# Order of decoding, early rows and early expert blocks in a two-layer block kernel on one core

## The chip, the cores and the metric

The kernel runs on one core of a Trainium2 chip, as one launch. Its time is the device time in microseconds (us); before the change it is 2848.39 us, the median of three runs (2846.98 to 2852.76). The engines are called by their names in the profile: PE multiplies matrices, PEld loads its weights, DVE does elementwise work on vectors, ACT evaluates activations, POOL (GpSimd) issues indirect transfers, SP issues the other transfers. All five run their own instruction queues, each in a fixed order.

## The reference

Two transformer blocks over 512 tokens of width 1024, in float32. The part that matters is the end of the first block, a layer that picks experts by product keys:

```
ada = silu(c) @ w_ada + b_ada            # 6 x 1024: shift1 scale1 gate1 shift2 scale2 gate2
x   = x + gate1 * mix                    # mix: attention and convolution, then w_out
h2  = rms_norm(x) * (1 + scale2) + shift2
q   = h2 @ w_query                       # 8 heads, two halves of 128
s1, s2 = scores of both halves against 128 keys each; top 16 of each
cand = 16 x 16 sums; top 16 -> expert index idx = 128*e1 + e2, gates = softmax
a   = gelu(h2 . peer_u[idx])             # 16384 experts, 8*16 = 128 per token
out = sum_k gates * a * peer_v[idx]
x   = x + gate2 * out
```

The second block (a long convolution, neighbourhood attention, pooling, and 16 experts) follows and is not touched.

## The kernel before, in words

`ada` is kept as 48 columns of 128. The first 16 are made by PE at the start. The other 32 (groups 8 to 23 of two columns each) are made by DVE in `ada_late` (L209): a group is a load of 1 MB into one of two `wada` tiles, two products with the row of `c` summed along the line (L219), and an addition of the bias (L223). Groups 8 to 19 run behind the four convolution groups (L366). Groups 20 to 23, which are gate2 (columns 40 to 47), are read for the first time at the very end of the expert layer (L778); they run after the eighth output block of `w_out` (L387). An output block is 24 matmuls, a bias and gate on ACT (L380), an addition to X (L381), a square on ACT and a sum on POOL. After them comes the norm of X (`rms_t`, L122 and L127), the column `gs2` (L468, which reads columns 32 to 39) and `modulate` (L164), whose steps are L166 on DVE, L167 and L168 on ACT, L169 on DVE.

In `peer` (L400 on) the 512 tokens are four tiles of 128. Tiles 0, 1 and 2 (384 tokens, `TD`) are done densely: all 128 blocks of 128 experts are scored for them, and the scores are weighted with a matrix of gates that is mostly zero. Tile 3 is done by gathering: for each of its tokens the 128 chosen rows of `peer_u`, then of `peer_v`, come by indirect transfers, 256 in all, each of 128 rows of 4 KB (L651).

- A *u unit* scores one block: load (L434), split into two parts (ACT L437, DVE L438), 24 matmuls of 384 columns (`u_matmuls`), then a Gelu. Each of the two parts has two buffers, the load has four.
- `queries` (L495) makes scores and their top 16 per head. `decode(t)` (L515) turns them into indices and gates of tile t, mostly on DVE; it is a generator that yields ten times. For tile 3 it writes `gidx` (L582) and `ggate`, for the others the rows e1T, e2T and gT.
- `spread(t)` (L593) lays the gates of a dense tile out as a matrix in eight *blocks* of 16 tokens. A block is 16 comparisons on DVE (L600), two more (L604), two copies on ACT (L605), 32 matmuls of 128 columns on PE (L609), four copies back (L611) and two stores to `Gd` (L613). It is called here the spread stage: 24 blocks.
- `early_u` (L618) does u units ahead of the main loop, and stores their Gelu in `Ad`. The blocks for it are those e with e mod 16 in `AHEAD` (L30): 40 of 128. Ten go between the yields of `decode(0)`, one into the step behind each spread block, the remaining six behind the stage. In the same step two yields of `decode(t + 1)` are taken.
- The main loop runs over e = 0 to 127 with an order written out by hand: a *v unit* (18 matmuls of 512 columns, `v_matmuls`) for each e, a u unit for those not done ahead, and `pace`, which puts gather steps between them in proportion to the units done. A gather step is an indirect transfer on POOL and a sum on DVE (L658 for `peer_u`, L664 for `peer_v`). The rows have five buffers in the pool `rp`, which is opened behind the spread stage.

Outside the main loop a planner sets each engine's order: by its own model of time it gives an engine the first instruction in program order whose operands and buffers are ready. An engine then keeps that order whatever happens on the chip.

Of the kernel before, what the change touches and what calls it, by code (L numbers as in the profile page):

```python
# [9 lines left out]
F32 = mybir.dt.float32  # L10
# [4 lines left out]
AF = mybir.ActivationFunctionType  # L15
ALU = mybir.AluOpType
# [4 lines left out]
P = 128  # L21
D = 1024
# [3 lines left out]
NEG = -1e30  # L26
LOW = -3e38
NDT = 3
TD = NDT * P
AHEAD = (1, 4, 7, 10, 13)  # L30
MAGIC = 12582912.0
TWO_PI_HI = 6.28125
TWO_PI_LO = 2.0 * math.pi - 6.28125
# [2 lines left out]
def body(ctx, tc, I, O):  # L36
    nc = tc.nc
    mm = nc.tensor.matmul
    act = nc.scalar.activation
    vtt = nc.vector.tensor_tensor  # L40
    vts = nc.vector.tensor_scalar
    stt = nc.vector.scalar_tensor_tensor
# [33 lines left out]
    def cols_of(name):  # L76
        o, n = CO[name]
        return cols[:, o:o + n]
# [98 lines left out]
    with ExitStack() as fx:  # L177
# [31 lines left out]
        def ada_late(gs, ins):  # L209
            ws_ = []  # L210
            for g in gs:
                w = fp.tile([P, 2, D], F32, name="wada", tag="wada", bufs=2)
                nc.sync.dma_start(w, I["w_ada_l"][g - KD])
                ws_.append((g, w))
                if len(ws_) == 2 or g == gs[-1]:
                    with tc.issue_after(ins.ins):
                        for g_, w_ in ws_:
                            for j in range(2):
                                stt(w_[:, j], w_[:, j], 1.0, cb, op0=ALU.mult, op1=ALU.mult,  # L219
                                    accum_out=ada[:, 2 * g_ + j:2 * g_ + j + 1])  # L220
                    ws_ = []
            b0, b1 = 2 * gs[0], 2 * gs[-1] + 2
            vtt(ada[:, b0:b1], ada[:, b0:b1], cols_of("b_ada")[:, b0:b1], op=ALU.add)  # L223
# [8 lines left out]
        with ExitStack() as ex:  # L232
# [8 lines left out]
            homes = [(ep, "dw")] * 4 + [(pmk, "sq")] * 2 + [(fp, "k_sb"), (fp, "v_sb"), (pmk, "sx")]  # L241
# [22 lines left out]
            for k in range(KD):  # L264
                if k + 2 < KD:
                    ada_group(k + 2, aw[k + 2])
                if k + 4 < KD:
                    aw.append(ada_load(k + 4))
                stt(gs1[:, k:k + 1], ada[:, 2 * k + 1:2 * k + 2], 1.0, cols_of("norm1_g")[:, k:k + 1],
                    op0=ALU.add, op1=ALU.mult)  # L270
# [101 lines left out]
        for i in range(KD):  # L372
            ps = mmp()
            hi, lo = wo.get(i)
            n = 0
# [3 lines left out]
            t = fp.tile([P, T], F32, name="mt", tag="mt", bufs=2)  # L379
            act(t, ps, AF.Identity, bias=gb1[:, i:i + 1], scale=ada[:, 16 + i:17 + i])  # L380
            ins = vtt(X[:, i], X[:, i], t, op=ALU.add)  # L381
# [2 lines left out]
                nc.gpsimd.tensor_copy(sx, sq)  # L384
            elif i < KD - 1:
                ptt(sx, sx, sq, op=ALU.add)
        ada_late(range(20, 24), ins)  # L387

    upx = ExitStack()
    up = upx.enter_context(tc.tile_pool(name="up", bufs=2))  # L390
    with ExitStack() as px:
        peer(px, tc, I, locals())
# [9 lines left out]
def peer(px, tc, I, E):  # L402
    nc = tc.nc
    mm = nc.tensor.matmul
    act = nc.scalar.activation
    vtt = nc.vector.tensor_tensor
    vts = nc.vector.tensor_scalar
    stt = nc.vector.scalar_tensor_tensor
# [9 lines left out]
    htm = kp.tile([P, D], F32, name="htm", tag="htm")  # L418
    gidx = kp.tile([P, P], I32, name="gidx", tag="gidx")
    ggate = kp.tile([P, P], F32, name="ggate", tag="ggate")  # L420
    e1T = kp.tile([P, TD], F32, name="e1T", tag="e1T")
    e2T = kp.tile([P, TD], BF16, name="e2T", tag="e2T")
    gT = kp.tile([P, TD], F32, name="gT", tag="gT")
    gs2 = kp.tile([P, KD], F32, name="gs2", tag="gs2")
    NBK = TD // 16
    Gd = [drp.tile([P, NBK, 64, 16], F32, name=f"Gd{c}") for c in range(2)]
    up = E["up"]
    papp = px.enter_context(tc.tile_pool(name="papp", bufs=2, space=PSUM))
    EARLY = [e for e in range(P) if e % 16 in AHEAD]
    Ad = drp.tile([len(EARLY), P, TD], F32, name="Ad")  # L430

    def u_split(e, lo_engine):
        raw = up.tile([P, KD, P], F32, name="uraw", tag="uraw", bufs=4)
        nc.sync.dma_start(raw, I["peer_uT"][e])  # L434
        hi = up.tile([P, KD, P], F32R, name="uhi", tag="uhi")
        lo = up.tile([P, KD, P], F32R, name="ulo", tag="ulo")
        act(hi, raw, AF.Copy)  # L437
        lo_engine.tensor_tensor(lo, raw, hi.bitcast(F32), op=ALU.subtract)  # L438
        return hi, lo

    def u_matmuls(hi, lo):
        ps = papp.tile([P, TD], F32, name="aps", tag="aps")
        for k in range(KD):
            mm3(ps, hi[:, k], lo[:, k], hh[:, k, :TD], hl[:, k, :TD], k == 0, k == KD - 1)
        return ps

    with ExitStack() as qx:
        gp = qx.enter_context(tc.tile_pool(name="gp", bufs=2))
# [144 lines left out]
        def spread(t, step):  # L593
            for blk in range(8 * t, 8 * t + 8):
                st = gp.tile([P, P, 16], F32, name="st", tag="st")
                for hb in range(2):
                    c0 = 16 * blk + 8 * hb
                    of = gp.tile([P, 8, P], F32, name="of", tag="of")
                    for j in range(8):
                        vts(of[:, j], iop, e1T[:, c0 + j:c0 + j + 1], gT[:, c0 + j:c0 + j + 1],  # L600
                            op0=ALU.is_equal, op1=ALU.mult)
                    oq = gp.tile([P, 8, P], F32, name="oq", tag="oq")
                    ob2 = gp.tile([P, P, 8], BF16, name="ob2", tag="ob2")
                    vtt(ob2, iob, e2T[:, None, c0:c0 + 8].to_broadcast([P, P, 8]), op=ALU.is_equal)  # L604
                    act(oq.rearrange("p t e -> p e t"), ob2, AF.Copy)  # L605
                    for t4 in range(2):
                        ps = pp.tile([P, 4, P], F32, name="gps", tag="gps")
                        for j in range(4):
                            mm(ps[:, j], oq[:, 4 * t4 + j], of[:, 4 * t4 + j], start=True, stop=True)  # L609
                        o = 8 * hb + 4 * t4  # L610
                        act(st[:, :, o:o + 4], ps.rearrange("p t e -> p e t"), AF.Copy)  # L611
                for c in range(2):
                    nc.sync.dma_start(Gd[c][:, blk], st[:, 64 * c:64 * c + 64])  # L613
                step()
# [3 lines left out]
        def early_u(count):  # L618
            for n in itertools.islice(early, count):
                gl = up.tile([P, TD], F32, name="gle", tag="gle", bufs=2)  # L620
                act(gl, u_matmuls(*u_split(EARLY[n], nc.vector)), AF.Gelu)  # L621
                nc.sync.dma_start(Ad[n], gl)
# [2 lines left out]
            queries(h)  # L625
        for _ in decode(0):
            early_u(1)
        for t in range(NDT):
            dec = decode(t + 1)

            def step():
                early_u(1)
                for _ in itertools.islice(dec, 2):
                    pass

            spread(t, step)
            for _ in dec:
                pass

    early_u(len(EARLY))  # L640

# [1 line left out]
    rp = px.enter_context(tc.tile_pool(name="rp", bufs=1))  # L643
    outp = rp.tile([P, D], F32, name="gacc", tag="gacc")
    nc.vector.memset(outp, 0.0)
    ga = rp.tile([P, P], F32, name="ga", tag="ga")
    scr = rp.tile([P, D], F32, name="gscr", tag="gscr")

    def gather(src, j):
        row = rp.tile([P, D], F32, name="row", tag="row", bufs=5)  # L650
        nc.gpsimd.indirect_dma_start(out=row, out_offset=None, in_=I[src],  # L651
                                     in_offset=bass.IndirectOffsetOnAxis(ap=gidx[:, j:j + 1], axis=0))
        return row

    def gather_step(n):
        if n < P:
            row = gather("peer_u", n)
            stt(scr, row, 1.0, htm, op0=ALU.mult, op1=ALU.mult, accum_out=ga[:, n:n + 1])  # L658
        else:
            if n == P:  # L660
                act(ga, ga, AF.Gelu)
                vtt(ga, ga, ggate, op=ALU.mult)
            row = gather("peer_v", n - P)
            stt(outp, row, ga[:, n - P:n - P + 1], outp, op0=ALU.mult, op1=ALU.add)  # L664

    ppo = px.enter_context(tc.tile_pool(name="ppo", bufs=1, space=PSUM))
    acc = [[ppo.tile([P, T], F32, name=f"acc{t}{c}", tag=f"acc{t}{c}") for c in range(2)] for t in range(NDT)]
    GG = 8
# [33 lines left out]
    def v_matmuls(e, wh, wl, vh, vl):  # L702
        for t in range(NDT):
            for c in range(2):
                mm3(acc[t][c], wh[:, t * P:(t + 1) * P], wl[:, t * P:(t + 1) * P],
                    vh[:, c * T:(c + 1) * T], vl[:, c * T:(c + 1) * T], e == 0, e == P - 1)

    total = 2 * P - len(EARLY)
    done = [0, 0]

    def pace(units):
        done[0] += units
        while done[1] < 2 * P and done[1] * total < done[0] * 2 * P:
            gather_step(done[1])
            done[1] += 1

# [8 lines left out]
    def u_mm(e):  # L725
        if e < P and e not in EARLY:
            ups[e] = u_matmuls(*usp.pop(e))
            return True
        return False
# [34 lines left out]
    for c in range(2):  # L764
        for t in range(4):
            cs = slice(c * T, (c + 1) * T)
            if t < NDT:
                st = rp.tile([P, T], F32, name="ot", tag="row", bufs=5)
# [775 lines left out]
```

## Time and profile before

| | us |
|---|---|
| median of three runs | 2848.39 |
| profiled execution, its own time | 2849.08 |
| its span (first to last instruction) | 2847.3 |
| PE busy | 2582.1 (91%) |
| DVE busy | 1457.3 (51%) |
| ACT busy | 917.3 (32%) |
| POOL busy | 495.1 (17%) |

The span holds the first block's mixer up to about 272 us, the norm and the queries up to 402 us, decoding and the spread stage up to 663 us, a tail of u units to 703 us, the main loop to 1591 us, and the second block to the end. Busy time is the union of an engine's instructions. The granted clock is that of PE, 1.00 for 2.4 GHz and 0.50 for 1.2 GHz.

### The profile page before, as it was taken

How to read it: one execution, taken by the hardware profiler on the slowest of the kernel's cores; microseconds unless marked ns; L12 is line 12 of the kernel's file. 1: busy time of each engine (PE TensorE's matmuls, PEld its weight loads, DVE VectorE, ACT ScalarE, POOL GpSimd, SP SyncE). 2: the span in 40 equal slices, each digit the busy share in tenths (PEclk: the TensorE clock that was granted, in tenths of full speed). 3: DMA queues.
4: the chain of work that ended last, by engine and by line, in shares of the span. 5: the costliest groups of instructions: out<-in, count | busy, mean ns of one | idle time of the engine just before them, and what ended most of it. 6: DMA issues, size and time to landing. Idle time of an engine off the chain costs nothing. (4 is left out here: it accounts for less than half of the span.)

```text
span 2847.3 us, 32895 instructions
## 1 busy us (share of the span) xinstructions
PE 2582.1 (91%) x12609; PEld 1813.7 (64%) x12609; DVE 1457.3 (51%) x2907; ACT 917.3 (32%) x1368; POOL 495.1 (17%) x342
## 2 busy tenths in 40 slices
PE   7998999988999999999999899969878888788887
PEld 5666788988988898888888777633323223233332
DVE  4485899994777877878778865330101101011011
ACT  4363448984333333333333434220000000000001
POOL 0001000001444544445444213010000000000000
PEclk9998999999999999999999999989999999999999
DMA  6343324556898989889988422279999999999997
GB/s 249 120 155 126 104 97 180 203 199 231 291 319 314 319 311 325 314 312 313 330 301 316 158 96 80 111 301 429 427 428 427 427 428 427 428 428 428 427 428 303
DMA packets 195077, 826.41 MB, mean 290 GB/s; under 512 B 17159, under 2 KB 77447, under 8 KB 167144
## 3 DMA queue, kind: packets, MB, share of 16 engines
q1 hardware_dynamic: 154280, 680.67, 61.0%
q0 software_dynamic: 38016, 138.43, 13.7%
q10 hardware_dynamic: 2624, 5.22, 0.5%
q8 instruction: 99, 1.62, 0.2%
q14 instruction: 58, 0.48, 0.0%
HBM read 787.02 MB, written 37.22 MB: 289 GB/s over the span
## 5 line engine op out<-in xcount | busy, mean ns | idle before, releaser
L1353 DVE TENSOR_TENSOR sg<-sg,upp 128x512 f32<-128x512 f32 x32 | 22.0, 688 | 754.3 <-PE upp L1346 754.3
L85 PE MATMUL aps<-hh,uhi 128*128 128x384 f32 x1024 | 347.8, 340 | 8.9 <-ACT gle L621 8.9
L87 PE MATMUL aps<-hh,ulo 128*128 128x384 f32 x1024 | 345.7, 338 | 5.1 <-DVE ulo L438 5.1
L86 PE MATMUL aps<-hl,uhi 128*128 128x384 f32 x1024 | 345.6, 337 | 0.0
L1346 PE MATMUL upp<-wch,XB 128*64 128x512 f32 x1024 | 274.2, 625 | 50.9 <-DMA wch<-in_w_up 50.9
L651 POOL DMA_INDIRECT row<-in_peer_u,gidx x128 | 205.2, 1603 | 628.7 <-issue 386.2
L85 PE MATMUL acc<-vh,wh 128*128 128x512 f32 x768 | 299.8, 390 | 2.4 <-ACT wh L81 2.4
L87 PE MATMUL acc<-vh,wl 128*128 128x512 f32 x768 | 300.2, 391 | 0.0
L86 PE MATMUL acc<-vl,wh 128*128 128x512 f32 x768 | 299.6, 390 | 0.4 <-DVE vl L82 0.4
L1346 PE MATMUL gp<-wch,XB 128*64 128x512 f32 x1024 | 268.0, 608 | 34.2 <-DMA wch<-in_w_gate 34.1
L1372 PE MATMUL y<-wch,aT 128*64 128x512 f32 x1024 | 247.7, 598 | 11.9 <-ACT aT L1358 11.9
L651 POOL DMA_INDIRECT row<-in_peer_v,gidx x128 | 207.4, 1621 | 240.3 <-DVE gacc L664 209.4
L1346 PEld LDWEIGHTS upp<-wch,XB 128*64 128x64 f32 x1024 | 86.7, 143 | 211.2 <-issue 141.7
L1346 PEld LDWEIGHTS gp<-wch,XB 128*64 128x64 f32 x1024 | 84.1, 140 | 198.7 <-issue 145.2
L437 ACT ACTIVATE uhi<-uraw 128x1024 fp32r<-128x1024 f32 x128 | 135.7, 1060 | 211.2 <-DMA uraw<-in_peer_uT 160.8
L85 PEld LDWEIGHTS aps<-hh,uhi 128*128 128x128 f32 x1024 | 194.0, 189 | 13.9 <-ACT gle L621 10.5
L87 PEld LDWEIGHTS aps<-hh,ulo 128*128 128x128 f32 x1024 | 193.6, 189 | 6.1 <-DVE ulo L438 6.1
L86 PEld LDWEIGHTS aps<-hl,uhi 128*128 128x128 f32 x1024 | 194.1, 190 | 4.1
L438 DVE TENSOR_TENSOR ulo<-uraw,uhi 128x1024 fp32r<-128x1024 f32 x128 | 156.2, 1221 | 73.4 <-ACT uhi L437 72.8
L1372 PEld LDWEIGHTS y<-wch,aT 128*64 128x64 f32 x1024 | 85.5, 136 | 141.3 <-issue 123.0
L1352 ACT ACTIVATE sg<-gp 128x512 f32<-128x512 f32 x32 | 19.1, 597 | 482.5 <-PE gp L1346 482.5
L664 DVE SCALAR_TENSOR_TENSOR gacc<-row,ga,gacc 128x1024 f32<-128x1024 f32 x128 | 164.1, 1282 | 2.4
(405 smaller groups left out, 4277.9 us busy)
## 6 DMA issues: line engine op xcount, KB each, us to landing
wch<-in_w_gate SPq DMA_DIRECT2D x64, 2048.0 KB, 35.4
wch<-in_w_up SPq DMA_DIRECT2D x62, 2048.0 KB, 32.9
wch<-in_w_down SPq DMA_DIRECT2D x62, 2048.0 KB, 34.4
uraw<-in_peer_uT SPq DMA_DIRECT2D x128, 512.0 KB, 7.6
vraw<-in_peer_v SPq DMA_DIRECT2D x128, 512.0 KB, 6.9
Gd<-st SPq DMA_DIRECT2D x48, 512.0 KB, 3.6
gg<-Gd SPq DMA_DIRECT2D x16, 1536.0 KB, 17.4
wraw<-in_w_in SPq DMA_DIRECT2D x36, 512.0 KB, 3.2
```

The costliest lines, as they stand in the source:

```text
L85: mm(out, lh, rh, start=first, stop=False)
L86: mm(out, lh, rl, start=False, stop=False)
L87: mm(out, ll, rh, start=False, stop=last)
L437: act(hi, raw, AF.Copy)
L438: lo_engine.tensor_tensor(lo, raw, hi.bitcast(F32), op=ALU.subtract)
L651: nc.gpsimd.indirect_dma_start(out=row, out_offset=None, in_=I[src], in_offset=bass.IndirectOffsetOnAxis(ap=gidx[:, j:j + 1], axis=0))
L664: stt(outp, row, ga[:, n - P:n - P + 1], outp, op0=ALU.mult, op1=ALU.add)
L1346: mm(ps[64 * e:64 * e + 64], xT[:, k, 64 * e:64 * e + 64], gu[w][e][:, o:o + T], start=k == 0, stop=k == KD - 1)
L1352: act(sg, ps2[0], AF.Silu)
L1353: vtt(sg, sg, ps2[1], op=ALU.mult)
L1372: mm(y[c][64 * e:64 * e + 64], aT[:, fb, 64 * e:64 * e + 64], dn[e][:, o:o + T], start=fc == 0 and fb == 0, stop=fc == 3 and fb == 3)
```

## The change

Three things. The groups 20 to 23 of `ada` are put behind the output blocks 1 to 4, one each, in place of behind the last. The decoding order is 0, 1, 3, 2, and two yields of it are taken in every step until it ends; from then on each step also does four gather steps, up to 40, and what is left of the 40 is done behind the stage. These rows have two buffers of their own in a pool `gr` that is opened before the stage, and the product is written over the row. Each step does two u units; `AHEAD` holds the eight odd residues, so 64 of 128 blocks are scored ahead: ten beside `decode(0)`, 48 in the 24 steps, six behind. The main loop has 64 u units and 216 gather steps left, and `pace` counts accordingly.

```
+NGE = 40
-AHEAD = (1, 4, 7, 10, 13)
+AHEAD = (1, 3, 5, 7, 9, 11, 13, 15)
@@ output blocks
-        ada_late(range(20, 24), ins)
+            if 0 < i < 5:
+                ada_late([19 + i], ins)
@@ peer
+    gr = px.enter_context(tc.tile_pool(name="gr", bufs=1))
+    ga = gr.tile([P, P], F32, name="ga", tag="ga")
+    sums, homes = [], [(gr, 2)]
+    def gather(src, j):
+        pool, bufs = homes[-1]
+        row = pool.tile([P, D], F32, name="row", tag="row", bufs=bufs)
...
+    def gather_step(n):
+        if n < P:
+            row = gather("peer_u", n)
+            stt(row, row, 1.0, htm, op0=ALU.mult, op1=ALU.mult, accum_out=ga[:, n:n + 1])
...
+        def decodes():
+            for t in (1, 3, 2):
+                yield from decode(t)
+                ended.append(t)
+        dec = decodes()
+        early_rows = iter(range(NGE))
+        def step():
+            early_u(2)
+            for _ in itertools.islice(dec, 2):
+                pass
+            if 2 in ended:
+                for n in itertools.islice(early_rows, 4):
+                    gather_step(n)
         for t in range(NDT):
-            dec = decode(t + 1)
-            def step():
-                early_u(1)
-                for _ in itertools.islice(dec, 2):
-                    pass
+            while t and t not in ended:
+                next(dec, None)
             spread(t, step)
-            for _ in dec:
-                pass
+        for n in early_rows:
+            gather_step(n)
@@ in front of the main loop
+    sums.append(outp)
+    homes.append((rp, 5))
-    done = [0, 0]
+    done = [0, NGE]
-        while done[1] < 2 * P and done[1] * total < done[0] * 2 * P:
+        while done[1] < 2 * P and (done[1] - NGE) * total < done[0] * (2 * P - NGE):
```

## Rows read from the trace of the kernel before

**Rows 1.** Busy time by stage: start:end length, engines, granted clock, DMA share, GB/s

```profile
402.00:452.00 50.00, 41.69 (x225) 39.67 (x225) 48.66 (x229) 28.66 (x34) 0.00 (x0) 0.97 0.35 121
452.00:663.00 211.00, 191.60 (x1329) 183.63 (x1329) 193.54 (x656) 186.08 (x206) 0.00 (x0) 0.99 0.54 198
663.00:703.00 40.00, 33.73 (x184) 33.09 (x182) 10.47 (x10) 12.07 (x18) 4.97 (x5) 0.96 0.72 257
703.00:1591.00 888.00, 887.22 (x4389) 795.18 (x4390) 696.88 (x855) 327.11 (x432) 407.64 (x251) 1.00 0.89 310
```

**Rows 2.** Waits of PE, 452 to 663 us: total us, times, longest

```profile
PE gps L609 <- ACT oq L605: 10.2, 10, 1.5
PE gps L609 <- ACT st L611: 7.9, 9, 1.6
```

**Rows 3.** Waits of PE, 703 to 1591 us

```profile
PE acc L85 <- ACT wh L81: 2.4, 2, 1.9
```

**Rows 4.** Timeline of DVE, output blocks and norm: start, duration, idle before

```profile
249.29 1.23 DVE L82 TENSOR_TENSOR wlo<-wraw,whi 128x1024 fp32r<-128x1024 f32 x1 [3.71 <-ACT whi L81]
...
272.20 1.22 DVE L219 SCALAR_TENSOR_TENSOR wada<-wada,c 128x1024 f32<-128x1024 f32 x1
...
276.78 0.17 DVE L122 RECIPROCAL rt<-rt 128x4 f32<-128x4 f32 x1
...
279.12 1.28 DVE L166 TENSOR_TENSOR mt<-X,rps 128x512 f32<-128x512 f32 x2 [0.81 <-PE rps L127]
...
285.11 0.16 DVE L468 SCALAR_TENSOR_TENSOR gs<-ada,cols 128x8 f32<-128x8 f32 x1
```

**Rows 5.** Timeline of ACT, the same norm

```profile
274.88 0.26 ACT L121 ACTIVATE rt<-nps,eps_t 128x4 f32<-128x4 f32 x1 [1.87 <-PE nps L119]
285.31 1.52 ACT L167 ACTIVATE mt<-mt,ada,gs 128x512 f32<-128x512 f32 x2 [10.16 <-DVE gs L468]
```

**Rows 6.** Timeline of PE, first product of the queries

```profile
289.55 0.79 PE L85 MATMUL mmp<-hh,uhi 128*128 128x512 f32 x1 [10.46 <-ACT uhi L81]
```

**Rows 7.** Timeline of ACT, u units one behind the other

```profile
665.60 1.06 ACT L437 ACTIVATE uhi<-uraw 128x1024 fp32r<-128x1024 f32 x1 [3.24 <-PE aps L86]
666.57 0.47 ACT L621 ACTIVATE gle<-aps 128x384 f32<-128x384 f32 x1
669.76 1.06 ACT L437 ACTIVATE uhi<-uraw 128x1024 fp32r<-128x1024 f32 x1 [2.72 <-PE aps L86]
```

**Rows 8.** Groups of DVE, 452 to 663 us: busy us, mean ns, idle before

```profile
L600 DVE TENSOR_SCALAR of<-iop,e1T,gT 128x128 f32<-128x128 f32 x384 | 103.7, 341 | 9.2 <-PE gps L609 8.8
L604 DVE TENSOR_TENSOR ob<-iob,e2T 128x1024 bf16<-128x1024 bf16 x48 | 32.4, 685 | 2.8 <-ACT oq L605 2.8
L438 DVE TENSOR_TENSOR ulo<-uraw,uhi 128x1024 fp32r<-128x1024 f32 x24 | 29.2, 1218 | 1.9 <-ACT uhi L437 1.8
```

**Rows 9.** Timeline of DVE, places from decoding to the first gathered rows

```profile
450.88 1.21 DVE L566 TENSOR_TENSOR oh<-oh,wb__3955 128x2048 bf16<-128x2048 bf16 x1
...
642.91 0.22 DVE L582 CAST gidx<-ef 128x128 int32<-128x128 f32 x1
...
706.94 1.22 DVE L658 SCALAR_TENSOR_TENSOR gscr<-row,htm 128x1024 f32<-128x1024 f32 x1
...
708.20 1.23 DVE L658 SCALAR_TENSOR_TENSOR gscr<-row,htm 128x1024 f32<-128x1024 f32 x1
```

**Rows 10.** Timeline of POOL, a row issued before and in the main loop

```profile
669.18 1.11 POOL L651 DMA_INDIRECT row<-in_peer_u,gidx  x1 [366.40 <-issue]
...
708.44 1.80 POOL L651 DMA_INDIRECT row<-in_peer_u,gidx  x1 [33.07 <-DVE gscr L658]
```

**Rows 11.** Line 651, all 256 rows, issue to landing

```profile
DMA to landing us min/median/max: 4.9/8.0/10.3
```

**Rows 12.** Transfers issued 452 to 663 us: KB each, median us to landing

```profile
uraw<-in_peer_uT SPq DMA_DIRECT2D x24, 512.0 KB, 3.4
```

**Rows 13.** Transfers issued 1100 to 1200 us

```profile
uraw<-in_peer_uT SPq DMA_DIRECT2D x10, 512.0 KB, 8.4
```

More of the change, by code (lines that the diff above doesn't have):

```diff
@@ L445, in u_matmuls @@
         return ps
+    gr = px.enter_context(tc.tile_pool(name="gr", bufs=1))
[4 more added lines that the diff above has]
+        row = pool.tile([P, D], F32, name="row", tag="row", bufs=bufs)
+        nc.gpsimd.indirect_dma_start(out=row, out_offset=None, in_=I[src],
+                                     in_offset=bass.IndirectOffsetOnAxis(ap=gidx[:, j:j + 1], axis=0))
+        return row
+    def gather_step(n):
+        if n < P:
+            row = gather("peer_u", n)
+            stt(row, row, 1.0, htm, op0=ALU.mult, op1=ALU.mult, accum_out=ga[:, n:n + 1])
+        else:
+            if n == P:
+                act(ga, ga, AF.Gelu)
+                vtt(ga, ga, ggate, op=ALU.mult)
+            row = gather("peer_v", n - P)
+            stt(sums[0], row, ga[:, n - P:n - P + 1], sums[0], op0=ALU.mult, op1=ALU.add)
     with ExitStack() as qx:
@@ L627, in peer @@
             early_u(1)
-        for t in range(NDT):
-            dec = decode(t + 1)
-            def step():
-                early_u(1)
-                for _ in itertools.islice(dec, 2):
-                    pass
+        ended = []
+        def decodes():
[11 more added lines that the diff above has]
+                    gather_step(n)
+        for t in range(NDT):
+            while t and t not in ended:
+                next(dec, None)
             spread(t, step)
-            for _ in dec:
-                pass
+        for n in early_rows:
+            gather_step(n)
     early_u(len(EARLY))
@@ L645, in peer @@
     nc.vector.memset(outp, 0.0)
[L646 to L664, printed above, removed]
+    sums.append(outp)
+    homes.append((rp, 5))
     ppo = px.enter_context(tc.tile_pool(name="ppo", bufs=1, space=PSUM))
```

## Prediction, made before the change was run

> **What bounds the kernel now.** I read the busy time by stage first, since the change moves work from one stage to another. The reader is to see in it that the main loop has no room on PE (887.22 of 888 us busy) and the three stretches ahead of it have some: 8.3 us idle in 402 to 452, 19.4 in the spread stage, 6.3 in the tail, 34.0 together [rows 1]. In the spread stage DVE is busy 92% of the time and ACT 88%, so PE's room there is not free for the asking. Next come PE's own waits. In the stage they are for the two copies on ACT that stand before and behind the matmuls of the gates, not for the u units [rows 2]; in the main loop there are 2.4 us of them [rows 3]. Last I read the timelines around the norm, where the third part of the change acts: DVE's products for the last `ada` groups begin as soon as X is done, and everything behind them queues [rows 4]. The sums below go against the profiled execution's 2849.08 us, 0.7 above the median of the runs.
>
> **Part 1: the `ada` groups.** Eight products of about 1.15 us each stand on DVE between the last X and `gs2`. The sequence is: ACT has the square root at 274.88 + 0.26 = 275.14 [rows 5], but DVE takes the reciprocal only at 276.78, behind four products; the norm's row comes 2.34 us later, at 279.12; then four more products, so that `gs2` is there at 285.11 [rows 4]. ACT has waited 10.16 us for it [rows 5], and PE starts the queries at 289.55 [rows 6]. Without the products the reciprocal runs at 275.2, L166 at 277.5, its first half ends at 278.2, and L167 (half of 1.52, 0.76) and L168 (about 0.6) give PE its operand at 279.6: 9.9 us earlier. PE's wait in rows 6 ends on the split of the query weights. That load could not start before the last product either, if its buffers lie where `wada` was; with the products early it falls away too. I take -9.5. The ends are -11, should the two splits also leave ACT's way, and 0, should the loads hold something else up.
>
> The products now stand behind output blocks 1 to 4. A group costs DVE 2 x 1.15 + 0.2 = 2.5 us there, and DVE idles 3.71 us in such a block before the next weight split [rows 4], so they are hidden. Without that cover four blocks would be late by up to 2.5 us each, 10 in all, which is the 0 end. SP gets the four loads of `wada` between the loads of `w_out`; a group's buffer comes free two groups before, and a block lasts 5.6 us, so nothing behind them on SP should be late.
>
> **Part 2: 24 u units out of the main loop.** Two neighbouring units start 4.16 us apart when PE alone paces them [rows 7]. The loop, PE-bound, loses 24 x 4.16 = 99.8 us, and the spread stage gains the same 99.8 us of PE work. So the move itself is worth nothing; what counts is how much of the 34.0 us of idle PE is filled, and what new idle arises. The 24 stores and loads of `Ad` and the `uraw` loads go along with the units.
>
> The spread stage afterwards: PE 191.6 + 99.8 = 291 us. DVE 193.5 + 24 x 1.22 + 40 rows x 1.26 (706.94 to 708.20) [rows 9] = 273. ACT 186.1 + 24 x (1.06 + 0.47) = 223 [rows 7]. PE is now the longest by 18 us, where before the three were within 8 us. A second u unit in each step also gives PE something to run while it waits for ACT's copies. I take it that the idle falls from 19.4 to about 8, a gain of 11, with ends of 0 (same idle) and 28 (all of the stage's, and most of the other stretches'). The other stretches I leave as they are: beside `decode(0)` DVE is 97% busy, and the tail runs the same six units.
>
> The rest of the main loop: 310 GB/s x 888 us = 275 MB move there now. The change takes out 24 loads of 0.524 MB and 40 rows of the same size, and adds 24 reads of 0.197 MB: 246 MB in 788 us, 313 GB/s, as before. Without the 40 rows it would be 339. So I cost the loop's remaining transfers at nothing; the cover is the same loads two elements ahead. The 40 sums taken from DVE there are worth nothing either, since DVE is not late in the loop.
>
> **Part 3: 40 rows in the stage.** This adds a wait of a new kind. DVE's order is fixed by the planner's model, and a sum whose row has not landed holds up all that is queued behind it on DVE: the comparisons of the next block, the low part of the next u unit, and by them ACT and PE. With two buffers a row can be issued only when the sum two before it is done. A buffer's cycle is 0.3 us to the issue, the landing, and 1.26 us of sum. The trace has no row in the spread stage. The landing lies between 4.9 and 10.3 us, median 8.0, all under the main loop's transfers or in the tail [rows 11]. Four rows take two cycles: 12.9 us at 4.9, 19.1 us at 8.0. A block with two u units takes PE 191.6 / 24 + 4.16 = 12.1 us. Over the nine steps that carry four rows each the price is 9 x 0.8 = 7 us at the short end, and 9 x 7.0 = 63 us at the median.
>
> Which end? A plain load of the same 512 KB lands in 3.4 us in the stage [rows 12] and 8.4 in the main loop [rows 13]. The stage will then carry more, about 270 GB/s in place of 198, so I put a row's landing there at 5.5 us: four rows in 14.1, 9 x 2.0 = 18 us. Against that stands that the planner does not keep to the steps: `decode(1)` is nearly through at 450.88, before the first comparison of the stage, though the program has it in the steps behind that [rows 9]. `gidx` came at 642.91, in block 21 of 24 [rows 9]; decoded second it comes in block 10 or 11. So 40 rows have some 14 blocks and the tail's 25 us, about 195 us or 4.9 each, while the buffers allow one in 3.5 (landing 5.5) to 4.8 (landing 8.0). I take 3 us of new stalls, nearer to the spread-out case, and keep 0 and 63 as ends. The last four rows stand beside the six units of the tail, where DVE is three quarters idle.
>
> One thing speaks against rows in this stage. POOL took 1.11 us for an issue when DVE was nearly idle and 1.80 with DVE busy [rows 10]; at 1.80 a cycle is 0.7 longer, inside the range above. The Trainium skill (SBUF — State Buffer, "Who interferes with whom") says that a DVE `tensor_scalar` can run in a mode that takes the port over which GpSimd writes the descriptors of its transfers, and that GpSimd is then blocked for the whole instruction; the 16 comparisons of a block (L600) are of that kind, and the main loop has none, so no run here shows it.
>
> **Sum.** -9.5 (part 1), -99.8 + 99.8 - 11 (part 2), +3 (part 3) = -17.5: 2849.1 - 17.5 = 2831.6, and 2831 from the median.
>
> **Rivals.**
>
> *The idle stays.* The stage keeps 19.4 us of idle, or gives back as much in stalls as it fills. For it: DVE stays at 91% and the order is fixed. Against it: the waits of rows 2 have no u unit beside them now. Then only part 1 is left: 2839.
>
> *All is filled.* PE has no idle in the stage and most of the other stretches' goes: -9.5 - 28 = 2811. For it: twice the u units as filler. Against it: beside `decode(0)` DVE sets the pace [rows 1].
>
> *The rows become the bound.* If the planner's model lands a row earlier than the chip does, sums are placed too early on DVE, and four rows a step at a landing of 6.5 us take 16.1: 9 x 4.0 = 36 us, with parts 1 and 2 2849 - 20.5 + 36 = 2865; at 8.0 it is 63, 2891. It decides from the landing at which 9 x (2 x (L + 1.56) - 12.1) = 20.5, which is L = 5.6 us. For it: two buffers in place of five, and a median of 8.0. Against it: 3.4 against 8.4 for the plain load, and the early start of the rows. This also covers the case that `gidx` comes late, so that the rows pile up in front of the loop.
>
> *Comparisons hold up the issue.* A block's 16 comparisons are 16 x 0.26 = 4.2 us in a row on DVE (103.7 / 384 = 0.27 each at the most [rows 8]). If an issue waits for such a run, a cycle at 4.9 is 10.7 us, four rows take 21.3, 9 x 9.2 = 83 us: 2849 - 20.5 + 83 = 2911. This is what the skill's page named above would bring at its worst; against it, each comparison ends in a quarter of a microsecond.
>
> **How the numbers follow.** Forecast 0.45 (2822 to 2838), idle stays 0.18, all filled 0.15, rows the bound 0.19, comparisons 0.03. A difference of 0.2%, 5.7 us, is about what can be told from none. Faster: 0.43 + 0.16 + 0.15 = 0.74. Within: 0.02 + 0.02 + 0.04 of the rows' case = 0.08. Slower: 0.15 + 0.03 = 0.18. The range 2806 to 2862 leaves out the rows' case above a landing of some 6.4 us (about 0.13), the last case, and a little of the third; the likeliest one's own range is 2822 to 2838.
>
> **What would show it.** Part 1: ACT's wait for `gs2` is gone and PE's first query product stands near 280; eight L219 products lie between 239 and 259 with no late weight split behind them. Part 2: the main loop lasts near 788 us with PE still full; the stretch from the first gate matmul to the last is near 295 us in place of 204. Part 3: sums of rows in the stage with landings near 5.5 us, and DVE waiting little for them. The prediction is wrong if DVE waits tens of microseconds for rows, if the main loop gets new PE waits, or if the products of part 1 reappear as a wait in the output blocks.

## The result, and the profile after

The changed kernel takes 2865.35 us (median of 5 runs, 2863.51 to 2866.47) against 2849.01 for the kernel before: a ratio of 1.0061, interval 1.005 to 1.0071. It is slower by 17 us; the forecast was 2831 and the range ended at 2862. The profiled execution took 2863.51 us, with a span of 2861.7.

I cut the span at the first `acc` product of the main loop, the first product of its v units (703.0 before, 816.8 after), and read busy time and clock ahead of it and in it. The columns are those of [rows 1], whose stretches answer to the last two rows. The kernel after:

```profile
0.00:290.00 290.00, 249.42 (x1260) 182.00 (x1261) 166.53 (x278) 132.38 (x231) 13.33 (x14) 0.94 0.47 170
290.00:402.00 112.00, 110.61 (x549) 91.26 (x548) 96.96 (x514) 45.01 (x79) 2.38 (x1) 0.99 0.22 76
402.00:816.80 414.80, 373.88 (x2305) 363.69 (x2303) 326.22 (x992) 262.13 (x305) 61.28 (x45) 0.96 0.66 233
816.80:1607.00 790.20, 788.20 (x3812) 694.60 (x3813) 616.09 (x752) 290.27 (x384) 318.35 (x211) 1.00 0.90 312
```

The loop lost 888.0 - 790.2 = 97.8 us and PE is still full in it, as forecast. It begins 816.8 - 703.0 = 113.8 us later. Together that is +16.0; the two spans differ by 14.4. So the loss is ahead of the loop. Between 402 us and the loop PE idles 414.80 - 373.88 = 40.9 us, where the rows of before add up to 34.0 [rows 1] and the forecast, 11 less and 3 more, to 26. It is also busy 106.9 us longer (373.9 against 267.0), where the forecast had 99.8 for the 24 units.

What DVE waits for from the first gate matmul to the last, 454 to 775 us (us in total, times, longest):

```profile
DVE row L463 <- DMA row<-in_peer_u,gidx: 47.5, 20, 4.6
```

And PE, in the same stretch:

```profile
PE aps L88 <- DVE ulo L440: 20.0, 8, 7.2
PE gps L633 <- ACT st L635: 5.5, 5, 2.6
PE gps L633 <- ACT oq L629: 4.7, 3, 2.6
```

The two waits of [rows 2] are smaller (7.9 to 5.5, 10.2 to 4.7), as the second u unit was to make them. The new line above them is larger than both were: PE waits for the low half of a u unit, which DVE makes, and DVE waits 47.5 us for rows. One place shows how they hang together. DVE in order of time (start, duration, idle before with its releaser):

```profile
616.95 1.23 DVE L463 SCALAR_TENSOR_TENSOR row<-row,htm 128x1024 f32<-128x1024 f32 x1
...
625.00 1.23 DVE L463 SCALAR_TENSOR_TENSOR row<-row,htm 128x1024 f32<-128x1024 f32 x1 [4.53 <-DMA row<-in_peer_u,gidx]
...
626.15 1.22 DVE L440 TENSOR_TENSOR ulo<-uraw,uhi 128x1024 fp32r<-128x1024 f32 x1
...
627.28 4.20 DVE L624 TENSOR_SCALAR of<-iop,e1T,gT 128x128 f32<-128x128 f32 x16
```

POOL issues a row in between:

```profile
618.46 1.68 POOL L456 DMA_INDIRECT row<-in_peer_u,gidx  x1 [5.92 <-DVE row L463]
```

The sum at 616.95 frees its buffer, POOL issues the next row into it at 618.46, and the sum of that row starts at 625.00: 6.5 us from issue to sum. DVE has stood idle for 4.53 of them, and the low half at 626.15 and the 16 comparisons of a block had to wait behind. The rows of the kernel after that are issued 520 to 660 us, from issue to landing:

```profile
DMA to landing us min/median/max: 4.7/6.4/10.4
```

The last step of the decoding, which lets them start, and the 40 sums (first and last start):

```profile
L606 DVE CAST gidx<-ef x1: 229/229/229, 524.6 to 524.6; 128x128 int32<-128x128 f32 x1
...
L463 DVE SCALAR_TENSOR_TENSOR row<-row,htm x40: 1206/1225/1234, 540.8 to 769.7; 128x1024 f32<-128x1024 f32 x40
```

`gidx` comes at 524.6 (642.91 before [rows 9]), and the sums stand over 229 us, so the rows have the time that the forecast gave them (195 us). In the median a row lands in 6.4 us and not in the 5.5 assumed.

The norm, on DVE:

```profile
273.06 0.17 DVE L492 SCALAR_TENSOR_TENSOR gs<-ada,cols 128x8 f32<-128x8 f32 x1
...
275.90 0.18 DVE L123 RECIPROCAL rt<-rt 128x4 f32<-128x4 f32 x1 [2.67 <-ACT rt L122]
...
280.32 1.23 DVE L83 TENSOR_TENSOR ulo<-uraw,uhi 128x1024 fp32r<-128x1024 f32 x1 [4.24 <-ACT uhi L82]
281.46 1.22 DVE L489 CAST stb<-start_row 128x2048 bf16<-128x2048 f32 x1
282.59 1.22 DVE L83 TENSOR_TENSOR ulo<-uraw,uhi 128x1024 fp32r<-128x1024 f32 x1
283.73 1.28 DVE L167 TENSOR_TENSOR mt<-X,rps 128x512 f32<-128x512 f32 x2
```

`gs` and the reciprocal are early, as forecast. But L167 (L166 before) starts at 283.73, 4.6 us later than before [rows 4]: two weight splits and the cast of `stb` stand ahead of it on DVE, and the first split waits for a load. ACT and PE:

```profile
279.23 1.06 ACT L82 ACTIVATE uhi<-uraw 128x1024 fp32r<-128x1024 f32 x1 [3.36 <-DMA uraw<-in_w_query]
284.45 1.52 ACT L168 ACTIVATE mt<-mt,ada,gs 128x512 f32<-128x512 f32 x2 [2.95 <-DVE mt L167]
...
288.50 1.52 ACT L168 ACTIVATE mt<-mt,ada,gs 128x512 f32<-128x512 f32 x2 [1.50 <-DVE mt L167]
...
302.10 0.58 ACT L528 ACTIVATE qT<-mmp 128x512 f32<-128x512 f32 x1
```

```profile
286.54 0.79 PE L86 MATMUL mmp<-hh,uhi 128*128 128x512 f32 x1 [8.33 <-ACT hh L169]
```

The first finished query block in the kernel before:

```profile
303.88 0.58 ACT L504 ACTIVATE qT<-mmp 128x512 f32<-128x512 f32 x1
```

PE starts the queries 3.0 us earlier than in [rows 6], not 9.9. L168 then runs in pairs every 4.05 us (284.45, 288.50), as DVE and ACT take turns on two columns at a time, and the first finished query block (L528) is at 302.10, 1.8 us earlier than before.

### The profile page after: what moved, and what is told of

Same layout as the page of the kernel before. It is cut to its first block, busy times and chain, and to the rows that moved or that the text cites. A ratio compares the mean times of both kernels' runs of the same rounds, so it can differ in the third digit from the quotient of the medians.

```text
span 2861.7 us, 33041 instructions
## 1 busy us (share of the span) xinstructions
PE 2588.9 (90%) x12609; PEld 1819.9 (64%) x12609; DVE 1455.0 (51%) x2910; ACT 916.7 (32%) x1368; POOL 462.6 (16%) x342
## 5 line engine op out<-in xcount | busy, mean ns | idle before, releaser
L456 POOL DMA_INDIRECT row<-in_peer_u,gidx x128 | 190.5, 1488 | 632.7 <-DVE row L463 358.5
L456 POOL DMA_INDIRECT row<-in_peer_v,gidx x128 | 189.1, 1477 | 281.5 <-DVE gacc L469 253.9
L463 DVE SCALAR_TENSOR_TENSOR row<-row,htm 128x1024 f32<-128x1024 f32 x128 | 153.5, 1221 | 47.5 <-DMA row<-in_peer_u,gidx 47.5
L82 ACT ACTIVATE vh<-vraw 128x1024 fp32r<-128x1024 f32 x128 | 134.7, 1053 | 130.2 <-PE acc L88 130.2
```

The costliest lines, as they stand in the source:

```text
L82: act(hi, src, AF.Copy)
L463: stt(row, row, 1.0, htm, op0=ALU.mult, op1=ALU.mult, accum_out=ga[:, n:n + 1])
```

## The experiments

Here `acc` is the start of the first `acc` product, "loop" the stretch from there to the loop's end, "row wait" the time DVE waits for rows ahead of the loop. Executions of one kernel differ by up to 12 us (e4: 2844.45 to 2856.21, its trace is of the slowest; e7's is of the fastest), so the two columns from single traces carry some us of that, and small differences are read from the ratios (against the kernel before on the same chip).

| kernel | acc | loop | row wait | median us | ratio (interval) |
|---|---|---|---|---|---|
| before | 703.0 | 888 | - | 2849.0 | |
| after | 816.8 | 790 | 47.5 | 2865.35 | 1.0061 (1.005 to 1.0071) |
| e1, no transfers | 799.8 | 788 | - | 2846.60 | 0.9999 (0.9991 to 1.0008) |
| e2, no early rows | 785.0 | 867 | - | 2910.21 | 1.0224 (1.0209 to 1.024) |
| e3, `ada` groups alone | 701.2 | 888 | - | 2843.80 | 0.9992 (0.9983 to 1.0001) |
| e4, four row buffers | 802.0 | 795 | 11.9 | 2848.44 | 1.0009 (0.9999 to 1.0019) |
| e5, `ada` groups and norm order | 698.0 | 889 | - | 2839.78 | 0.9973 (0.9962 to 0.9985) |
| e6, rows alone | 777.3 | 886 | 45.4 | 2920.67 | 1.0252 (1.0238 to 1.0266) |
| e7, norm order and six buffers | 789.6 | 788 | 6.0 | 2839.99 | 0.9971 (0.996 to 0.9982) |
| e8, twenty rows | 791.7 | 823 | 19.1 | 2872.02 | 1.0089 (1.0076 to 1.0103) |

My theory after the result: two row buffers and a landing of 6.4 us make DVE wait, and what queues behind it on DVE holds up PE. The rivals: the 40 sums are too much for DVE whatever the transfers do; the u units cost more than they give back; the `ada` groups lose somewhere else.

**e1: the sums without their transfers.** The first 40 sums are made from a constant tile; the transfers of these rows are left out, so these sums are not the reference's.

```diff
 def gather_step(n):
+    if n < NGE:
+        stt(stills[1], stills[0], 1.0, htm, op0=ALU.mult, op1=ALU.mult, accum_out=ga[:, n:n + 1])
+        return
```

> The changed kernel with the first 40 rows not gathered: their 40 sums run on DVE at the same places in the program, but over a constant tile that lies in SBUF all along (the transfers of these 40 rows are left out, and so the sums of tile 3 are not those of the reference). Theory A, the landing of the rows holds DVE: in the changed kernel DVE waits 47.5 us for rows and the stage from the first gate matmul (454.3) to the last (774.9) lasts 320.6 us in place of 204.4. Then the stage falls to 290 to 302 us, DVE's waits for rows are 0, and the time is 2838 to 2848. Rival B, DVE has too much to do in the stage (the 40 sums are 50 us of it): the stage stays above 312 us and the time above 2857. Rival C, the second u unit in each step costs it: as B, above 2857.

Measured: 0.9999, against 1.0061 with the transfers, inside the range of theory A. So the transfers and what hangs on them cost about 0.6%, 17.7 us by the two ratios. But the experiment is not clean. Without `gidx` to wait for, 17 of the 40 sums moved forward into the scoring of the queries. The group of these sums, 290 to 402 us, then the stretches of e1:

```profile
L466 DVE SCALAR_TENSOR_TENSOR still<-still,htm 128x1024 f32<-128x1024 f32 x17 | 20.8, 1225 | 1.1 <-ACT htm L512 0.9
```

```profile
290.00:402.00 112.00, 102.07 (x475) 82.10 (x474) 102.49 (x469) 38.76 (x69) 2.40 (x1) 0.95 0.20 66
402.00:799.80 397.80, 374.05 (x2378) 364.92 (x2376) 320.45 (x1036) 267.48 (x314) 5.52 (x5) 0.99 0.54 193
```

PE idles 9.9 us in the first of them, where it idles 1.4 in the kernel after. The sums that stay in e1 have a price too, so the 17.7 us are a lower bound of what the early rows cost.

**e2: no early rows at all.** The u units and the `ada` groups stay; all 256 rows go to the main loop.

```diff
-NGE = 40
+NGE = 0
```

> The changed kernel with no early rows at all: all 256 are gathered in the main loop, the 64 early blocks, the order of decoding and the ada groups stay as changed. Theory A: the stage lasts 288 to 300 us as without the transfers; the main loop has to move 268 MB in 790 us, 339 GB/s, and is the question: at no cost the time is 2838 to 2848, and if it becomes bound by transfers it is later by its new PE waits. Rival B (DVE's load by the sums): stage 285 to 295, since 50 us of DVE work is gone; it differs from the run without transfers by 10 us or more. Rival C (the u units): stage above 312, time above 2857.

```profile
0.00:290.00 290.00, 249.61 (x1272) 182.46 (x1273) 168.71 (x282) 133.86 (x233) 13.33 (x14) 0.95 0.48 170
290.00:402.00 112.00, 110.08 (x552) 90.56 (x550) 97.50 (x530) 45.15 (x78) 2.39 (x1) 1.00 0.24 78
402.00:785.00 383.00, 362.19 (x2287) 354.44 (x2287) 278.93 (x891) 260.16 (x303) 5.42 (x5) 0.98 0.55 197
785.00:1652.00 867.00, 817.43 (x3815) 710.43 (x3816) 662.21 (x831) 290.54 (x385) 405.92 (x251) 0.97 0.89 308
```

This measures parts 1 and 2 ahead of the loop: it begins at 785.0, 82.0 us later than before, where the forecast's terms give 99.8 - 20.5 = 79.3. PE's idle between 402 us and the loop falls from 34.0 to 20.8, by 13 where 11 was forecast. And it gives the price of the 40 early rows: 816.8 - 785.0 = 31.8 us. Of these 19.8 are idle PE (82.9 against 63.1 ahead of the loop) and 12.0 are longer matmuls (733.9 busy against 721.9, for 4114 and 4111 matmuls, while the granted clock is 0.96 and 0.98 from 402 us to the loop). The stage lasts 288.6 us, as theory A and rival B both had it, so e2 alone doesn't tell them apart.

The loop is the other half. It lasts 867 us, so with 64 u units and all its rows PE no longer sets its pace. What PE, and then ACT, wait for in it (785 to 1652 us):

```profile
PE acc L86 <- ACT wh L82: 51.1, 17, 4.7
...
ACT uhi L439 <- DMA uraw<-in_peer_uT: 169.7, 46, 9.0
```

And ACT in the loop of the kernel before:

```profile
ACT uhi L437 <- DMA uraw<-in_peer_uT: 160.8, 74, 7.9
```

ACT's wait alone shows nothing, since before it was nearly as long while PE was full. What speaks for the transfers is the rate: 308 GB/s, what the loop moved before [rows 1], not the 339 that the forecast named for this case and left unpriced. With 20 rows fewer (e8) the loop lasts 823, with 40 fewer 790: 1.6 to 2.2 us for each row, and a row of 0.524 MB at 308 GB/s is 1.7. The units can't leave the loop without the rows.

**e3: the `ada` groups alone.** The kernel before with

```diff
+if 0 < i < 5:
+    ada_late([19 + i], ins)
```

> The kernel before with only the last ada groups moved behind output blocks 1 to 4. My prediction gave this -9.5 us: 2839.5. What the trace of the changed kernel shows speaks for less: the wait for gs2 is gone, but the first query result is copied out at 302.10 in place of 303.88, since the load of the query weights starts only at 272.99 and two of DVE's instructions stand behind it, ahead of L166. By that it is -1 to -3, 2846 to 2848.

0.9992: some 2 us (-1 to -3 expected), and none is not excluded. PE's first query product, and on ACT the first finished query block:

```profile
286.86 0.79 PE L85 MATMUL mmp<-hh,uhi 128*128 128x512 f32 x1 [8.29 <-ACT hh L168]
```

```profile
302.43 0.58 ACT L505 ACTIVATE qT<-mmp 128x512 f32<-128x512 f32 x1
```

They stand where the kernel after has them (286.54, 302.10). So part 1 is the same with or without the rest, and short by itself.

**e4: four row buffers.** The odd rows take the place of `keysT`, which is done with by then and is cut into two tiles of a row's size.

```diff
+        if len(homes) == 1 and j % 2:
+            row = homes[0][2].tile([P, D], F32, name="row", tag="keysT", bufs=2)
...
+        keysT = [qp.tile([P, 8, P], F32, name="keysT", tag="keysT", bufs=2) for _ in range(2)]
```

> The changed kernel with four row buffers in the stage: odd rows lie where the keys were, which are read for the last time in the queries. Theory A (landing against two buffers): a row can be issued four sums ahead, so DVE's waits for rows fall from 47.5 to under 12 us, the stage lasts 292 to 305, the time is 2840 to 2852. If the planner places the sums closer together because it counts on the buffers too, the waits stay above 25 us and the time above 2857; then it is the planner's idea of the landing and not the number of buffers. Rival B (DVE's load): above 2857 with small waits.

```profile
DVE row L466 <- DMA row<-in_peer_u,gidx: 11.9, 9, 3.3
...
L466 DVE SCALAR_TENSOR_TENSOR row<-row,htm x40: 1206/1223/1227, 544.6 to 706.9; 128x1024 f32<-128x1024 f32 x40
```

DVE's wait falls from 47.5 to 11.9 and the time to 1.0009, 15 us less than after by the two ratios; both are within what theory A expected. The number of sums and transfers is the kernel after's. The planner's order is not: the sums stand within 162 us in place of 229. So the wait falls though the sums stand closer, and it is the buffers and not a wider spacing that take it away. The theory holds in part: the two buffers are about half of the 31.8 us.

**e5: the norm put in order.** The kernel before, with the `ada` groups of e3 and three edits in the norm: the first two modulations ahead of the splits in the program, the cast behind the queries, and four `mt` buffers. It is without the u units and the early rows.

```diff
-        nc.vector.tensor_copy(stb, start_row[:, :, None].to_broadcast([P, 16, P]))
...
+            for k in range(2):
+                modulate(k, r2, gs2[:, k:k + 1], ada[:, 24 + k:25 + k], hh, hl, n2, 4)
             wq0 = [wq.get(half) for half in range(2)]
...
+        nc.vector.tensor_copy(stb, start_row[:, :, None].to_broadcast([P, 16, P]))
```

> The kernel with only the ada groups moved, and three things in the norm behind them: the first two modulations stand ahead of the splits of the query weights in the program, the cast of start_row stands behind the norm, and modulate has four buffers in place of two. Theory: the forecast 9.9 us of part 1 failed because DVE's order puts two weight splits, whose load starts only when X is done (272.99, landing 279.2), and the cast ahead of L166, and because two buffers make DVE and ACT take turns (4.06 us for two columns). Then PE's first query product comes at 280 to 282 and the first query result at 294 to 297 in place of 302.10, and the time is 5 to 8 us below that of the ada groups alone (2843.8): 2836 to 2839. Rival: the weights' load and the slow clock after the gap set the pace; then the first result stays at 300 or later and the time within 2 us of the ada groups alone.

```profile
280.04 1.06 ACT L81 ACTIVATE uhi<-uraw 128x1024 fp32r<-128x1024 f32 x1 [3.41 <-DMA uraw<-in_w_query]
...
292.37 1.14 ACT L168 ACTIVATE hh<-mt 128x512 fp32r<-128x512 f32 x2
...
298.64 0.58 ACT L508 ACTIVATE qT<-mmp 128x512 f32<-128x512 f32 x1
```

0.9973, 7.7 us under the kernel before on the same chip by the ratio, and 5.4 us below e3. The last operand is done at 292.37 + 1.14 (in the kernel after at 299.2) and the first query block at 298.64, 5.2 us earlier than the 303.88 of before. I had expected more of the start: PE's first product is at 285.07 (280 to 282 expected), because the split at 280.04 still waits for the query weights and one split still stands ahead of L166 on DVE (281.12, 282.27). The three edits were not run one by one, nor without the `ada` groups.

**e6: rows alone.** One u unit in each step as before, 40 early rows as after.

> The changed kernel with one u unit a step and 40 early blocks as before, but with the 40 rows in the stage. Theory A (two buffers against the landing): a block is then 8.7 us of PE, and the rows in it still need 4 x 4 us; DVE's waits for rows are 40 us or more, the stage is longer than before by 45 to 70 us (50 of DVE's sums, which was 92% busy, and waits), and the main loop, bound by PE, gives nothing back: 2890 to 2920. Rival C (the second u unit is the cost in the changed kernel): the stage is longer by less than 25 us, and the time is below 2870.

```diff
-AHEAD = (1, 3, 5, 7, 9, 11, 13, 15)
+AHEAD = (1, 4, 7, 10, 13)
...
         def step():
-            early_u(2)
+            early_u(1)
```

1.0252: 72 us, and 2920.67 lies just above theory A's 2920. The loop takes 886 us with 40 rows fewer, so without the units' leaving they are worth nothing there. The loop begins 74.3 us later:

```profile
402.00:777.30 375.30, 294.72 (x1743) 280.60 (x1741) 302.39 (x986) 231.37 (x258) 47.25 (x45) 0.90 0.62 211
```

PE's idle between 402 us and the loop is 80.6 us, 46.6 more than before, and the same matmuls take 294.7 us at a granted clock of 0.90 where the rows of before have 267.0 at 0.96 to 0.99 [rows 1]. The waits and the landing:

```profile
DVE row L463 <- DMA row<-in_peer_u,gidx: 45.4, 31, 6.8
...
PE gps L633 <- ACT oq L629: 56.7, 27, 6.2
```

```profile
DMA to landing us min/median/max: 4.1/5.4/9.8
```

A row lands here in 5.4 us, about what the forecast assumed (5.5), and DVE waits as long as in the kernel after; but its sums stand closer, 604.6 to 758.9, one in 4.0 us. PE's wait for `oq` is 46.5 us longer than in [rows 2]. Not all of it is the stall: from 402 us to the loop DVE is busy 49.7 us longer than before (302.4 against 252.7), which is the sums, and idle 24.6 longer. DVE was 92% busy in the stage, so here its load (rival B) weighs as well, and e6 doesn't separate the two. The same rows cost 31.8 us beside two units a step: the second unit seems to hide part of what they cost.

**e7: norm order and six buffers**, the version to which e4 and e5 point: the changed kernel with e5's edits, and rows by turns in three pairs of buffers (the places of the keys and of the query results, cut to a row's size).

```diff
+        if len(homes) == 1 and j % 3:
+            row = homes[0][2].tile([P, D], F32, name="row", tag=("keysT", "qT")[j % 3 - 1], bufs=2)
```

> The changed kernel with the norm as in the run before last and six row buffers in the stage (rows also lie where the keys and the query results were). Theory A: DVE's waits for rows are under 5 us (11.9 with four), the stage 290 to 300, and with the norm's 6 us the time is 2834 to 2842, faster than the kernel before. Rival: what is left is the planner's order, then the waits are small and the time still above 2846.

```profile
DVE row L466 <- DMA row<-in_peer_u,gidx: 6.0, 5, 2.4
```

```profile
DMA to landing us min/median/max: 5.8/8.7/11.0
```

DVE's wait is down to 6.0 us, 1.0 above the forecast for it, although a row now takes 8.7 us to land: more transfers are open at a time, each slower, and the wait goes all the same. The ratio is 0.9971, some 8 us below the kernel before. But e5, without units and early rows, has 0.9973, so the move itself still earns nothing that can be told from none.

**e8: twenty rows**, two in each step.

```diff
-NGE = 40
+NGE = 20
...
-    for n in itertools.islice(early_rows, 4):
+    for n in itertools.islice(early_rows, 2):
```

> The changed kernel with 20 early rows, two a step, in place of 40. Without early rows the stage lasts 288.6 us and the main loop 867; with 40 it is 320.6 and 790. Theory A: half the rows have time to land, so DVE waits under 15 us for them and the stage lasts 294 to 306. The main loop then gathers 236 rows at 331 GB/s; if its cost grows steadily with the rows it lasts 820 to 835 and the time is 2870 to 2890; if there is a threshold it lasts under 800 and the time is 2840 to 2855.

```profile
791.70:1614.50 822.80, 798.82 (x3813) 697.62 (x3814) 636.66 (x792) 288.64 (x384) 347.76 (x231) 0.99 0.90 312
```

1.0089, as expected for a cost that grows with the rows. The stage is relieved (the loop begins 25 us earlier than after), but the loop, with 20 rows more, gives back 33. DVE waits 19.1 us for the 20 rows, where I had expected less than 15: the pair of buffers holds it up even at half the rows.

## Why the prediction was wrong

**The step that failed is in part 3:** "so 40 rows have some 14 blocks and the tail's 25 us ... I take 3 us of new stalls, nearer to the spread-out case". The early rows cost 31.8 us (e2 against after), so this term holds 29 of the 34 us between 2831 and 2865. By the starts and lengths of the loop the others are +7.7 (part 1), -5.0 and +2.0 (part 2).

Two things were wrong in the term. The landing was 6.4 us and not 5.5. And the argument compared averages: one row in 4.9 us wanted, one in 3.5 to 4.8 allowed. The rows did spread as I said, 40 sums over 229 us, one in 5.9, or one in 4.7 without the waits. But they came in bursts: of the 47.5 us of waits, 28.7 lie at the 17 sums between 600 and 680 us. Without these waits the 17 are wanted one in 3.0 us ((80 - 28.7) / 17), where two buffers allow one in 4.0 at a landing of 6.4 ((6.4 + 1.56) / 2). Slack in one block doesn't pay for a burst in another, as DVE's order is fixed. The landing alone isn't it: in e6, at 5.4, DVE waits 45.4 us, with its sums wanted one in 2.8 us.

**The rival "The rows become the bound" had the mechanism.** At a landing of 6.5 us it gave 36 us of stalls and 2865; 31.8 and 2865.35 were measured, at 6.4. That the two times agree so closely is in part luck: it took part 1 for -9.5 and part 2 for -11, and of the 31.8 us it had no term for the 12.0 of longer matmuls. Its working, four rows in two buffer cycles against the 12.1 us of a block, was the better model, and I had it on the page. e6 does not test it: the same working (two cycles of 5.4 + 1.56 against a block of 8.0) gives 9 x 5.9 = 53, and the loop began 74 later, but the working leaves out the sums' own 49.7 us on DVE. A chance of 0.19 was too little for a mechanism whose break-even, 5.6, lay 0.1 us above a landing that no row showed.

Not all of the price is the buffers'. With four the ratio falls by 0.52%, 15 us. With six some 8 to 14 us remain: by the single traces 4.6 us by the start of the loop (e7 against e2), plus what the norm's order gives, 701.2 - 698.0 = 3.2 by the same start and 5.4 by the ratios of e3 and e5; by the ratios e7 and e5 are even, so all of the 14.0 us that part 2 earns (97.8 - 83.8) is used up. Whether that is the load of the sums on DVE or the rows' share of the transfers, no run tells.

**Part 1** was over-sized: -9.5 forecast, about -2 measured (e3), with none not excluded. The step that failed is "L166 at 277.5"; it started at 283.73. I took the eight products out of DVE's queue and let the norm move up, but not what else was queued there. The weight splits and the cast came to stand ahead of L167, and the splits wait for a load that SP issued at 272.99:

```profile
272.99 11.18 SPq L100 DMA_DIRECT2D uraw<-in_w_query  x6
```

The forecast had taken that load as early too. Together with three edits in the norm the groups' move is worth 7.7 us by the ratio (e5); what the norm's order is worth without it was not run. The products as such are hidden behind the output blocks, as forecast: from the weight split at 236.23 to the last X at 272.26 it is 36.0 us, before (235.57 to 271.59) as long.

**Part 2** was right, and a little better than forecast. The loop lost 98 us (99.8), the units and the decoding order put 83.8 us ahead of it (785.0 - 701.2; forecast 88.8), and PE's idle fell by 13 (11). That the loop's remaining transfers cost nothing holds with 40 rows out of it (790), not with 20 (e8) or none (e2).

**"Comparisons hold up the issue"** did not show for the issue itself. In e6 one began inside a run of comparisons. DVE, then POOL:

```profile
626.01 2.17 DVE L624 TENSOR_SCALAR of<-iop,e1T,gT 128x128 f32<-128x128 f32 x8
```

```profile
626.37 0.94 POOL L456 DMA_INDIRECT row<-in_peer_u,gidx  x1 [1.06 <-DVE row L463]
```

It ended at 627.31, inside the run, and took 0.94 us, where the shortest issue of the stage took 0.93. The issues that took 1.68 us and more stand beside a sum or a low half of a u unit on DVE.

For the landing it stays open. Of the 40 early rows of the kernel after, the 12 with more than 4 us of comparisons in the first 6 us behind their issue landed in 8.0 us in the median, the other 28 in 6.1; in e8 it is 7.7 and 6.0, in e4 8.5 and 7.3, in e7 8.7 and 8.6. Whether the comparisons or the loads beside them did that, no run tells.

## What to carry to other kernels

A consumer in an engine's fixed order with N buffers gets at most N tiles in each cycle of issue, landing and use; compare that with the densest block that wants them, not with the average over the stage, and price the burst. Where a landing isn't in the trace, the case that hangs on it deserves as much chance as the favourable one. When you take work out of a queue, list what is left there ahead of the instruction that you hope to see earlier, and who feeds it.

## What the runs showed of the hardware

A row's landing goes with what is open beside it: 5.4 us in e6 (0.62 DMA share from 402 us to the loop), 6.4 after (0.66), 8.7 with six buffers (0.69).

The second product of an `ada` group took 2.31 us where its neighbour took 1.21, beside a sum on POOL. DVE and POOL of the kernel after:

```profile
240.95 1.21 DVE L220 SCALAR_TENSOR_TENSOR wada<-wada,c 128x1024 f32<-128x1024 f32 x1
242.09 2.31 DVE L220 SCALAR_TENSOR_TENSOR wada<-wada,c 128x1024 f32<-128x1024 f32 x1
```

```profile
241.85 1.47 POOL L387 TENSOR_TENSOR sx<-sx,sq 128x512 f32<-128x512 f32 x1 [1.37 <-ACT sq L134]
```

The sum ends at 243.32, and the product 1.08 us after that, nearly a whole product's time. In each of the four groups the second product takes 2.31 or 2.32 us beside such a sum; before, with nothing on POOL beside them, all eight took 1.22. The Trainium skill (SBUF — State Buffer, "Who interferes with whom") says that a DVE instruction with two inputs from SBUF contends with a GpSimd instruction that reads SBUF; these places agree, with 1.1 us lost in each. The forecast put these products at 1.15 us each; the output blocks hid the rest.

PE's stalls came with slower matmuls: in e6 46.6 us more of idle between 402 us and the loop went with 27.7 us of longer matmuls, at a granted clock of 0.90; in the kernel after, against e2, 19.8 went with 12.0, at 0.96 and 0.98.
